# A row-sum kernel whose first buffer is filled by two loads, one row and then fifteen, rather than by one

## The chip, the cores and the metric

The kernel runs on one core of one Trainium2 chip (trn2). The metric is the device time of one execution in microseconds (us), lower is better. Before the change it was 163.97 us, the median of three runs (163.81 to 164.09).

## The reference

```python
batch, seq, dim = 32, 512, 1024            # x: float32, 67.1 MB
def reference(x):
    return np.sum(x, axis=-1).astype(np.float32)
```

Each of 16,384 rows of 1,024 numbers is summed. There is one addition per four bytes read, so the question is how fast 67.1 MB can be brought into the core's memory (SBUF).

## The kernel before

Each of the 128 partitions owns 128 consecutive rows. They are handled in eight tiles of 16 rows per partition (64 KiB per partition, 8 MiB per tile), in three rotating buffers. The vector engine (DVE) sums half of the rows of a tile in one instruction, the scalar engine (ACT) the other half row by row. The queue of SyncE (SP) issues all the loads.

```python
    def load(xt, c0, a, b):
        nc.sync.dma_start(out=xt[:, a:b], in_=x_p[:, c0 * D + a : c0 * D + b])
    # rows_dve: one tensor_reduce over n rows; rows_act: one activation with accumulation per row
    ...
    for t in range(T - 1):                        # seven whole tiles, G = 16 rows each
        c0 = t * G
        xt = xpool.tile([P, G * D], F32, tag="xt", name="xt")     # bufs=3
        load(xt, c0, 0, G * D)
        rows_dve(xt, c0, 0, G // 2)
        rows_act(xt, c0, G // 2, G // 2)
    # the last tile: loads of 8, 4, 2, 1 rows and three parts of a row, so that little work is left at the end
    ...
```

## Time and profile before

| what | number | read in |
|---|---|---|
| time | 163.97 us | runs |
| span of the profiled run | 162.4 us | page |
| busy: DVE, ACT | 69.9 us, 69.0 us | page, part 1 |
| whole tiles readable, steady part | every 19.36 us | timeline |
| one 8 MiB tile in 19.36 us | 8.389 MB / 19.36 us = 433 GB/s | worked out |

These are lines of the page of the kernel before: busy time per engine with its share of the span, the load queue (packets, MB, share of the time of 16 DMA engines), the chain of waits by engine, and the two costliest groups (busy us, mean ns of one, then idle time before them and what ended it).

```profile
DVE 69.9 (43%) x16; ACT 69.0 (43%) x129; POOL 0.2 (0%) x4
...
q1 hardware_dynamic: 2160, 67.18, 96.3%
...
DMA 85%; DVE 11%; SPq 1%; issue 1%; DVEq 0%
...
L43 DVE TENSOR_REDUCE res<-xt 128x8 f32<-128x8192 f32 (+3 forms) x10 | 68.7, 6873 | 89.0 <-DMA xt<-in_x_dram 89.0
L53 ACT ACTIVATE xt<-xt 128x1024 f32<-128x1024 f32 x64 | 66.7, 1043 | 89.3 <-DMA xt<-in_x_dram 89.1
```

Both compute engines are idle for more than half of the span, and it is a load that ends nearly all of it. The pace of the loads stands in the timeline of DVE before the change (start us, duration us, engine, line, operation, and in brackets the idle time before it and its releaser). Each line starts when a tile has landed.

```profile
22.97 8.69 DVE L43 TENSOR_REDUCE res<-xt 128x8 f32<-128x8192 f32 x1 [22.97 <-DMA xt<-in_x_dram]
42.27 8.69 DVE L43 TENSOR_REDUCE res<-xt 128x8 f32<-128x8192 f32 x1 [10.62 <-DMA xt<-in_x_dram]
...
100.73 8.69 DVE L43 TENSOR_REDUCE res<-xt 128x8 f32<-128x8192 f32 x1 [10.72 <-DMA xt<-in_x_dram]
120.09 8.69 DVE L43 TENSOR_REDUCE res<-xt 128x8 f32<-128x8192 f32 x1 [10.67 <-DMA xt<-in_x_dram]
139.44 8.69 DVE L43 TENSOR_REDUCE res<-xt 128x8 f32<-128x8192 f32 x1 [10.66 <-DMA xt<-in_x_dram]
```

From 100.73 to 120.09 and on to 139.44 is 19.36 and 19.35 us, of which DVE works 8.69. The Trainium skill (DMA: Bandwidth & Descriptors, section "Where 436 GB/s comes from") gives 435 GB/s as the ceiling of the path into SBUF; this trace's 433 GB/s agrees. In its middle the stream is therefore full.

The waits of SP's queue in the same kernel (what waited, for what: us in total, times, longest):

```profile
SPq L40 <- DVE res L43: 105.8, 5, 29.6
SPq L40 <- DMA xt<-in_x_dram: 7.8, 1, 7.8
```

The queue waits for a free buffer with two tiles of loads still in front of it: the time from issue to landing of a whole tile is 49.4 us, over two and a half tiles.

### The profile page before, as it was taken

The numbers are of one execution on the slowest core, as the hardware profiler recorded it, in microseconds if no ns is written. First come the engines' busy times: TensorE is split into PE (matmuls) and PEld (weight loads), VectorE is DVE, ScalarE is ACT, GpSimd is POOL, SyncE is SP. The second block draws the span as 40 slices with busy tenths as digits, with TensorE's granted clock in tenths as the row PEclk, the third lists the DMA queues.
The fourth block names the chain that finished last, engine by engine and source line by source line (L and its number), as shares of the span: only waits on it lengthen the run. The fifth ranks groups of instructions, "written<-read, shape, count | busy, mean of one in ns | idle before, by whom it ended". The sixth has DMA issues, their size and how long they took to land.

```text
span 162.4 us, 220 instructions
## 1 busy us (share of the span) xinstructions
DVE 69.9 (43%) x16; ACT 69.0 (43%) x129; POOL 0.2 (0%) x4
## 2 busy tenths in 40 slices
DVE  0000039700595007940099101990049700697882
ACT  3000039700594007930099101990039600696881
POOL 0000000000000000000000000000000000000000
DMA  7979989989989989989997997997997997999980
GB/s 258 517 323 452 517 355 420 517 371 404 501 355 436 517 371 404 517 371 404 517 452 325 517 468 307 517 468 323 501 484 323 484 484 307 452 420 408 418 350 20
DMA packets 2161, 67.18 MB, mean 414 GB/s; under 512 B 240, under 2 KB 624, under 8 KB 880
## 3 DMA queue, kind: packets, MB, share of 16 engines
q1 hardware_dynamic: 2160, 67.18, 96.3%
q14 instruction: 1, 0.01, 0.0%
HBM read 67.11 MB, written 0.07 MB: 414 GB/s over the span
## 4 chain that ended last, share of the span: by engine, by line
DMA 85%; DVE 11%; SPq 1%; issue 1%; DVEq 0%
DMA xt<-in_x_dram 85%; DVE res L43 11%; SPq L40 1%; DVE xt L62 0%; DVE part L62 0%; DVEq L62 0%; DVEq L128 0%
## 5 line engine op out<-in xcount | busy, mean ns | idle before, releaser
L43 DVE TENSOR_REDUCE res<-xt 128x8 f32<-128x8192 f32 (+3 forms) x10 | 68.7, 6873 | 89.0 <-DMA xt<-in_x_dram 89.0
L53 ACT ACTIVATE xt<-xt 128x1024 f32<-128x1024 f32 x64 | 66.7, 1043 | 89.3 <-DMA xt<-in_x_dram 89.1
L53 ACT ACTIVATION_READ_ACCUMULATOR xt<-xt 128x1 f32 x64 | 11.9, 187 | 0.0
L53 ACT ACT_TABLE_LOAD x1 | 1.3, 1283 | 0.7 <-PEq L117 0.7
L62 DVE CUSTOM_DVE_ANT_0 xt<-xt 128x256 f32<-128x256 f32 x1 | 0.4, 425 | 0.9 <-DMA xt<-in_x_dram 0.9
L62 DVE CUSTOM_DVE_ANT_0 xt<-xt,part 128x128 f32<-128x128 f32 x2 | 0.7, 352 | 0.1
L62 DVE DVE_READ_ACCUMULATOR2_ANT part<- 128x1 f32 x2 | 0.2, 82 | 0.0
L117 POOL MEMSET const-bfloat16-1.0<- 128x1 bf16 x1 | 0.1, 101 | 0.0
L117 POOL MEMSET const-uint8-127<- 128x1 uint8 x1 | 0.1, 101 | 0.0
L117 POOL MEMSET const-float32-0.0<- 128x1 f32 x1 | 0.1, 98 | 0.2 <-issue 0.2
L117 POOL MEMSET const-float32-1.0<- 128x1 f32 x1 | 0.1, 98 | 0.0
L62 DVE DVE_READ_ACCUMULATOR2_ANT res<- 128x1 f32 x1 | 0.1, 84 | 0.0
## 6 DMA issues: line engine op xcount, KB each, us to landing
xt<-in_x_dram SPq DMA_DIRECT2D x1, 4096.0 KB, 39.7
xt<-in_x_dram SPq DMA_DIRECT2D x1, 2048.0 KB, 44.2
xt<-in_x_dram SPq DMA_DIRECT2D x1, 1024.0 KB, 46.2
xt<-in_x_dram SPq DMA_DIRECT2D x1, 512.0 KB, 47.0
xt<-in_x_dram SPq DMA_DIRECT2D x1, 256.0 KB, 47.1
xt<-in_x_dram SPq DMA_DIRECT2D x2, 128.0 KB, 43.0
xt<-in_x_dram SPq DMA_DIRECT2D x7, 49.4
out_dram<-res SPq DMA_DIRECT2D x1, 64.0 KB, 1.5
```

Source lines behind the costliest of these rows:

```text
L40: nc.sync.dma_start(out=xt[:, a:b], in_=x_p[:, c0 * D + a : c0 * D + b])
L43: nc.vector.tensor_reduce(out=res[:, c0 + j : c0 + j + n], in_=xt[:, j * D : (j + n) * D].rearrange("p (j d) -> p j d", d=D), axis=mybir.A ...
L53: nc.scalar.activation(out=v, in_=v, func=mybir.ActivationFunctionType.Copy, accum_out=res[:, c0 + i : c0 + i + 1],)
L62: nc.vector.tensor_tensor_reduce(out=xt[:, a : a + h], in0=xt[:, a : a + h], in1=xt[:, a + h : b], scale=1.0, scalar=first, op0=ADD, op1=A ...
L117: nc = _bacc.Bacc("TRN2", target_bir_lowering=False, num_devices=1)
```

## The change

The first whole tile is loaded as row 0 and then rows 1 to 15. The intent of such a change is that something arrives early. The code after the loads is the same.

```diff
     for t in range(T - 1):
         c0 = t * G
         xt = xpool.tile([P, G * D], F32, tag="xt", name="xt")
-        load(xt, c0, 0, G * D)
+        if t:
+            load(xt, c0, 0, G * D)
+        else:
+            load(xt, c0, 0, D)
+            load(xt, c0, D, G * D)
         rows_dve(xt, c0, 0, G // 2)
         rows_act(xt, c0, G // 2, G // 2)
```

## The prediction

> **What bounds the kernel now.** The input stream bounds it. In the timeline, the full 8 MiB tiles become readable at 42.27, 61.96, 81.33, 100.73, 120.09 and 139.44 us, which in the steady part is 19.36 us apart: 8.389 MB / 19.36 us = 433 GB/s. The trace's packet records say the same of one engine: a 65,536-byte packet (one partition of one tile) takes 2.42 us, 27.1 GB/s, back to back, on 16 engines. This agrees with the 435 GB/s ceiling that the Trainium skill gives (DMA: Bandwidth & Descriptors, section "Where 436 GB/s comes from"), so the stream has nothing left to gain in its middle. The chain of waits gives 85% of 162.4 us to the loads. The reductions are short beside them: the table of groups has DVE 69.9 us and ACT 69.0 us busy, with 8.69 us of vector work per tile of 19.36 us; both engines stand idle for 89 us waiting for loads. With three buffers the loads are queued two to three tiles ahead (issue to landing: 49 us), so the issuing engine, whose waits for free buffers look long (105.8 us), holds nothing up.
>
> The ends of the stream: the first packets start about 1.7 us into the span, the 16 engines start over 1.17 us, and their first packets take 2.55 to 3.41 us rather than 2.42. The last load is read at 158.6 us and about 3.8 us of tail follow.
>
> **What the change does.** Same bytes, same reductions, one load more. The first 128 packets of 64 KiB become 128 packets of 4 KiB and 128 of 60 KiB. The first reduction on DVE reads rows of both loads and the ACT rows lie in the second, so no reduction can start before the whole first tile has landed. No work starts earlier, and the hidden reductions would not shorten the stream if it did.
>
> Costs:
> - One more issue on the queue of SP, 0.33 to 0.50 us in the timeline. The second load's issue should be over at about 1.6 us, before the first packet even starts; an engine has 8 small packets, at 0.16 us each 1.3 us, plus 0.5 to 1 us of first-packet delay, to hide it. No gap expected: 0 us.
> - Per-packet overhead. A 4 KiB packet took 0.160 us in the tail against 0.151 us at the steady rate, so 8 of them cost about 0.08 us more per engine; one more completion packet costs about 0.01 us. The timeline agrees: the tail's load of one row arrived about 1.28 us after the load before, against 19.36 / 16 = 1.21 us. All this is on the critical path: +0.1 us.
> - Semaphores: the loads rotate over a few; the last tile's last piece before waited 7.8 us on a landing. It shifts by one load and keeps some 38 us of lead: 0 us.
>
> **Predicted.** 163.97 + 0.1 = 164.1 us, range 163.7 to 164.6. Chances: faster by over 2% 0.01, within 2% 0.97, slower by over 2% 0.02.
>
> **What would show it.** One load issue more, at about 1.2 us; 2,304 packets in the load queue rather than 2,160; first reduction at 22.97 + 0.1 = about 23.1 us; all later arrivals 19.36 us apart and shifted by the same 0.1 us; DVE and ACT busy times unchanged; small packets at the start with no gap of over 0.3 us on an engine before its first 60 KiB packet.
>
> **What would make it wrong.** The second load's descriptors arriving late, which leaves every engine idle for up to 1 us at the start (+0.5%). The 60 KiB packets being cut into many smaller ones (up to +0.1 us per 8 cuts). A start with short packets that loses less of the first-packet delay would give back 0.5 us. None reaches 2%.

## The result, and the profile after

The changed kernel took 163.93 us (median of 4 runs, 163.86 to 164.08), the kernel before 163.95 us in its 4 runs. The ratio is 1.000 with a 95% interval of 0.9983 to 1.0017: the same.

The lines of the page after the change:

```profile
DVE 69.9 (43%) x16; ACT 69.0 (43%) x129; POOL 0.2 (0%) x4
...
q1 hardware_dynamic: 2304, 67.18, 96.5%
...
DMA 85%; DVE 11%; SPq 2%; issue 1%; DVEq 0%
```

Busy times are unchanged, the load queue has 2,304 packets (2,160 before: a packet is a piece that the records list with its own start, size and duration, here one partition's part of one load; 128 of the 144 more carry data, 16 have four bytes and mark the end of the added load), and the chain is the same but for the issue of one load more. The issue of the second load shows as its own piece in the chain of waits, in order of time, after the change (start us, us, what); it is over at 1.58 us:

```profile
0.73 0.38 SPq L40
1.11 0.05 issue
1.16 0.43 SPq L40
```

The timeline of DVE after the change:

```profile
22.88 8.69 DVE L43 TENSOR_REDUCE res<-xt 128x8 f32<-128x8192 f32 x1 [22.88 <-DMA xt<-in_x_dram]
42.18 8.69 DVE L43 TENSOR_REDUCE res<-xt 128x8 f32<-128x8192 f32 x1 [10.61 <-DMA xt<-in_x_dram]
...
100.75 8.69 DVE L43 TENSOR_REDUCE res<-xt 128x8 f32<-128x8192 f32 x1 [10.87 <-DMA xt<-in_x_dram]
120.10 8.69 DVE L43 TENSOR_REDUCE res<-xt 128x8 f32<-128x8192 f32 x1 [10.66 <-DMA xt<-in_x_dram]
139.44 8.69 DVE L43 TENSOR_REDUCE res<-xt 128x8 f32<-128x8192 f32 x1 [10.66 <-DMA xt<-in_x_dram]
```

The first tile came 0.09 us earlier, not 0.1 us later as predicted; by the fifth tile the two kernels are level. Nor were the arrivals in between 19.36 us apart, as predicted: after the second tile they came 19.56, 19.45 and 19.56 us apart. So the total fits, but not yet the reasons. One trace cannot decide about 0.1 us, so the experiments repeat both kernels, multiply the suspected cost, and move the small load.

### The profile page after: what moved, and what is told of

Same layout as the page of the kernel before. It is cut to its first block, busy times and chain, and to the rows that moved or that the text cites. A ratio compares the mean times of both kernels' runs of the same rounds, so it can differ in the third digit from the quotient of the medians.

```text
span 162.3 us, 224 instructions
## 1 busy us (share of the span) xinstructions
DVE 69.9 (43%) x16; ACT 69.0 (43%) x129; POOL 0.2 (0%) x4
## 3 DMA queue, kind: packets, MB, share of 16 engines
q1 hardware_dynamic: 2304, 67.18, 96.5%
## 4 chain that ended last, share of the span: by engine, by line
DMA 85%; DVE 11%; SPq 2%; issue 1%; DVEq 0%
DMA xt<-in_x_dram 85%; DVE res L43 11%; SPq L40 2%; DVE xt L62 0%; DVE part L62 0%; DVEq L62 0%; DVEq L132 0%
```

## The experiments

Four theories stood against each other. A: the prediction, a small cost per packet, all on the critical path, and nothing gained. B: the short packets also lose less at the start of the stream, and about 0.2 us comes back. C: splits cost nothing anywhere. And the reading that the change invites: an early first row lets work begin early.

To see the start closely, the packet records of each profile were added up as follows: 15 us after the first packet, how many bytes have landed (a packet in flight counts in proportion), and how much longer did that take than at 433.6 GB/s, the steady 27.1 GB/s of 16 engines? This "deficit" is in us; the same at 150 us shows what was lost on the whole way. These are own calculations from the records, one execution per line of the table, not lines of the profile.

| kernel | first load, then | deficit at 15 us | at 150 us | ratio to the kernel before (95% interval) |
|---|---|---|---|---|
| before, first trace | 16 rows | 1.04 | 1.21 | |
| before again | 16 rows | 1.14 | 1.24 | 1.0004 (0.9990 to 1.0019) |
| DVE work doubled | 16 rows | 1.13 | 1.20 | 0.9999 (0.9985 to 1.0013) |
| order reversed | 15 rows, 1 row | 1.14 | 1.22 | 0.9994 (0.9980 to 1.0007) |
| halves | 8 rows, 8 rows | 1.12 | 1.33 | 1.0001 (0.9988 to 1.0014) |
| two rows first | 2 rows, 14 rows | 0.85 | 1.11 | 0.9991 (0.9977 to 1.0005) |
| changed, first trace | 1 row, 15 rows | 0.86 | 1.40 | 1.0000 (0.9983 to 1.0017) |
| changed, second | 1 row, 15 rows | 0.90 | 1.18 | 0.9984 (0.9972 to 0.9997) |
| changed, third | 1 row, 15 rows | 1.09 | 1.12 | 0.9985 (0.9973 to 0.9998) |
| row 0 reduced early | 1 row, 15 rows | 0.88 | 1.44 | 0.9981 (0.9968 to 0.9995) |
| all seven tiles split | 1 row, 15 rows | 0.91 | 1.46 | 1.0014 (1.0001 to 1.0026) |
| ramp | 1, 2, 4, 9 rows | 1.27 | 1.54 | 1.0000 (0.9986 to 1.0014) |
| quarter row first | 1/4 row, 15 3/4 rows | 1.49 | 1.56 | 1.0022 (1.0009 to 1.0035) |
| sixteen loads | 16 times 1 row | 1.73 | 2.21 | 1.0116 (1.0084 to 1.0149) |

All outputs are right. The first four new runs shared one chip and its runs of the kernel before, likewise the next four and the last four.

### The kernel before, once more

No edit. The noise floor.

> The unchanged kernel once more, as the noise floor. Every theory: ratio 1.000 to the kernel before within 0.1%. Its packet records also show how much the loss in the first packets (0.53 us per engine in the first profile, beyond 2.42 us a packet) and the scattered long packets in the middle of the stream (0.16 us per engine) vary from one execution to the next. If the middle varies by 0.3 us or more with the same kernel, the longer middle of the changed kernel (0.54 us) is no effect of the change.

Measured: 164.11 us against 164.05 us, ratio 1.0004. The profiles of one and the same kernel put the first tile at 22.97 and 23.17 us, so a single first-tile time says nothing about 0.1 us. The deficit at 15 us was 1.04 and 1.14, and between 15 and 150 us 0.17 and 0.10 us were added: the middle varied by less than 0.1 us, not by 0.3 us. The three profiles of the changed kernel vary far more there, from 0.03 to 0.54 us, so by that measure too the longer middle of the first one is no sure effect of the change.

### The changed kernel, twice more

No edit against the changed kernel.

> The changed kernel once more, with more rounds. Theory A (the prediction): per-packet overhead of eight 4 KiB packets and one completion per engine, +0.08 to +0.1 us, all on the critical path, ratio 1.0005. Theory B: the short packets also lose less at the start, since the first-packet delay is paid beside a short packet instead of a long one, and give back 0.2 us: ratio 0.9990 to 1.0000, and the mean engine finishes the first tile 0.1 to 0.2 us earlier than in the kernel before, as it did in the first profile (20.38 against 20.22 us after the first packet). If that early finish doesn't repeat, B falls.

Measured: 163.88 us, ratio 0.9984 (0.9972 to 0.9997).

> The changed kernel a third time, beside the order-reversed one. The first 4 runs gave ratio 1.000, six more 0.9984 (0.9972 to 0.9997). Theory A in its recorded size (+0.08 to +0.1 us): 1.0005. Theory A with the size that the kernel with all tiles split shows (a split tile arrives 19.42 us after the one before against 19.36 us, so +0.06 us): 1.0004. Theory B (a gain of 0.2 us or more at the start on top): 0.9985 to 0.9995. At a noise of 0.1% a ratio of 0.9985 again would speak for B, one of 1.000 or more would leave nothing to explain.

Measured, on another chip: 163.82 us, ratio 0.9985 (0.9973 to 0.9998). Two calls of two agree on -0.15%, which is -0.25 us, while the first four runs showed 0.00%. The early finish of the first tile repeated in the deficit of the second profile (0.90) and hardly in the third (1.09). The gain of theory B is likely but small, and well inside what counts as the same.

### All seven whole tiles split

```diff
-        load(xt, c0, 0, G * D)
+        load(xt, c0, 0, D)
+        load(xt, c0, D, G * D)
```

> All seven whole tiles are loaded as 1 + 15 rows, not the first one alone. Theory A: each split costs 0.08 us more of stream (eight 4 KiB packets at 0.1595 us against 0.1511 us each, and a completion packet of 0.015 us), so seven cost +0.6 us: 164.5 us, ratio 1.0035. Theory B (gain at the start): six extra splits of the middle get nothing back, so +0.5 us over the changed kernel and +0.4 us over the kernel before. Theory C (the splits cost nothing anywhere, since the stream's pace is set by something other than packets): ratio 1.000.

Measured: 164.31 us, ratio 1.0014 (1.0001 to 1.0026). Theory A's +0.6 us is outside; nothing at all (C) is outside too, barely. Theory B's +0.4 us over the kernel before (ratio 1.0024) is inside. Against the changed kernel of the same call, six splits more cost 164.34 - 163.86 = 0.48 us in the means. The DVE timeline of this kernel gives the price of a split:

```profile
22.66 8.69 DVE L43 TENSOR_REDUCE res<-xt 128x8 f32<-128x8192 f32 x1 [22.66 <-DMA xt<-in_x_dram]
42.07 8.69 DVE L43 TENSOR_REDUCE res<-xt 128x8 f32<-128x8192 f32 x1 [10.73 <-DMA xt<-in_x_dram]
61.49 8.69 DVE L43 TENSOR_REDUCE res<-xt 128x8 f32<-128x8192 f32 x1 [10.73 <-DMA xt<-in_x_dram]
80.93 8.69 DVE L43 TENSOR_REDUCE res<-xt 128x8 f32<-128x8192 f32 x1 [10.75 <-DMA xt<-in_x_dram]
100.72 8.69 DVE L43 TENSOR_REDUCE res<-xt 128x8 f32<-128x8192 f32 x1 [11.11 <-DMA xt<-in_x_dram]
```

A split tile follows its predecessor by 19.41 and 19.42 us, where an undisturbed whole one takes 19.36: about 0.06 us per split, not the 0.08 to 0.1 us predicted. Of the four that follow, three came after 19.42 to 19.44 us and one after 19.79 us, a hiccup of the kind that the kernel before has too (19.69 us between 42.27 and 61.96). Six splits at 0.06 us are 0.36 us; the other 0.12 us of the 0.48 lie within the noise of these means (0.13% of 164 us is 0.2 us).

### The first tile in sixteen loads

```diff
         ...
+        else:
+            for r in range(G):
+                load(xt, c0, r * D, (r + 1) * D)
         ...
```

> The first tile is loaded as 16 loads of one row, 15 of them added. Theory A: 128 packets of 4 KiB per engine at 0.0084 us too much each make 1.07 us, 15 completions 0.2 us: +1.3 us, 165.2 us; with theory B's gain of 0.2 us at the start +1.1 us. Theory C: 0. If the issues of the loads (0.43 us each on the queue of SP, at most eight loads in flight) were what counts, gaps between packets of an engine would show in the first 20 us and the loss would be above 1.5 us.

Measured: 166.14 us, but spread from 164.99 to 166.91; ratio 1.0116. The profiled run was one of the shorter, 165.34 us. In its ACT timeline each row is taken up as it lands:

```profile
20.21 1.06 ACT L53 ACTIVATE xt<-xt 128x1024 f32<-128x1024 f32 x1
...
21.48 1.06 ACT L53 ACTIVATE xt<-xt 128x1024 f32<-128x1024 f32 x1
...
22.77 1.06 ACT L53 ACTIVATE xt<-xt 128x1024 f32<-128x1024 f32 x1
```

A row arrives every 1.28 us, against 19.36 / 16 = 1.21 us: 0.07 us per one-row load, and again somewhat less than the prediction's 0.09. The deficit gives less: between 10 and 15 us after the first packet, in which four rows' packets started, it grew by 0.17 us, 0.04 us per row. Sixteen such loads explain at most about 1.1 of the 1.9 us between the means (166.03 and 164.11). The rest is something else: between 5 and 15 us after the first packet the deficit grew from 0.93 to 1.73 us, and in that stretch the packet records hold 19 packets of 4 KiB that took 0.21 to 0.84 us instead of 0.16. What they took too long sums to 7.9 us, over 16 engines 0.49 us. SP did wait for landings before it could issue more (14 times, 65.4 us in the whole execution), but the records show no time there with fewer than 16 packets in flight, so the gap that a late issue would leave isn't seen, although the loss is above the 1.5 us that was expected of it. What makes these packets long, and why the runs of this kernel scatter by 1.9 us, stays open.

### The same two loads in the other order

```diff
         ...
+        else:
+            load(xt, c0, D, G * D)
+            load(xt, c0, 0, D)
         ...
```

> The same two loads of the first tile in the other order: 15 rows first, then the one row. Same packets, same count. Theory A: no different from the changed kernel, +0.06 us, ratio 1.0004. Theory B: the gain at the start needs the short packets to be the first, so it is gone here: 0.06 us slower than the kernel before and 0.2 to 0.3 us slower than the changed kernel in the same call (ratio to before 1.0004, while the changed kernel has 0.9985); the mean engine finishes the first tile as late after the first packet as in the kernel before (20.38 and 20.48 us) plus 0.06, not at 20.22.

Measured: 163.97 us, all five runs between 163.94 and 163.99; ratio 0.9994 (0.9980 to 1.0007). Its deficit at 15 us, 1.14 us, is that of the kernel before. The packets are the same as in the changed kernel, only their order differs, so in these traces the early gain goes with the order: it is there when the short packets come first. One trace of this order doesn't prove it, since the third trace of the changed kernel, at 1.09 us, is nearly as late. In time the difference to the changed kernel of the same call is 163.97 - 163.83 = 0.14 us in the means, less than the 0.2 to 0.3 us expected and not clear of the noise. The start of the packet records tells the same story: the first 60 KiB packets of this kernel took 2.86 to 3.30 us instead of 2.27.

### Row 0 reduced as soon as it lands

```diff
         ...
+            load(xt, c0, 0, D)
+            load(xt, c0, D, G * D)
+            rows_dve(xt, c0, 0, 1)
+            rows_dve(xt, c0, 1, G // 2 - 1)
         ...
```

> The changed kernel with the first reduction on DVE cut into row 0 alone and rows 1 to 7, so that row 0 is reduced as soon as its own load has landed: the first reduction starts at about 4.5 us rather than 22.9. If starting work early were worth something, the 1.2 us of that reduction would be gained: ratio 0.993. Theory of the prediction (the loads bound it and the reductions are hidden): the early start gains nothing, every later arrival stays 19.36 us apart, ratio 1.000 within 0.2% and no different from the changed kernel.

Measured: 163.80 us, ratio 0.9981 (0.9968 to 0.9995), which isn't to be told from the changed kernel's 0.9985. The DVE timeline of this kernel shows what the early start is worth:

```profile
4.15 1.22 DVE L43 TENSOR_REDUCE res<-xt 128x1 f32<-128x1024 f32 x1 [4.15 <-DMA xt<-in_x_dram]
22.71 7.62 DVE L43 TENSOR_REDUCE res<-xt 128x7 f32<-128x7168 f32 x1 [17.35 <-DMA xt<-in_x_dram]
42.08 8.69 DVE L43 TENSOR_REDUCE res<-xt 128x8 f32<-128x8192 f32 x1 [11.74 <-DMA xt<-in_x_dram]
```

The first reduction starts 18.7 us earlier than in the changed kernel. DVE then merely waits 17.35 us for the next load, and before the second tile it is idle for 11.74 us rather than 10.61: the work done early comes back as waiting. Early work is worth nothing here.

### The DVE work of six tiles done twice

```diff
         load(xt, c0, 0, G * D)
+        if t < 6:
+            rows_dve(xt, c0, 0, G // 2)
         rows_dve(xt, c0, 0, G // 2)
```

> The kernel before with the 8.69 us reduction on DVE done twice in six of the seven whole tiles (the second overwrites the first with the same sums), 52 us of work more. If the reductions were on the critical path, as the 11% of the chain of waits given to that line might be read, the time rises by up to 52 us. Theory of the prediction: 17.4 us of vector work per tile still fits under the 19.36 us between tiles, only the free buffer comes 8.7 us later and the loads are queued two tiles ahead: ratio 1.000 within 0.2%, arrivals still 19.36 us apart.

Measured: 164.05 us, ratio 0.9999. The page of this kernel (busy time per engine, then the chain of waits by engine) and its DVE timeline:

```profile
DVE 122.0 (75%) x22; ACT 69.0 (43%) x129; POOL 0.2 (0%) x4
...
DMA 74%; DVE 22%; SPq 1%; issue 1%; DVEq 0%
```

```profile
61.85 17.41 DVE L43 TENSOR_REDUCE res<-xt 128x8 f32<-128x8192 f32 x2 [1.95 <-DMA xt<-in_x_dram]
81.20 17.41 DVE L43 TENSOR_REDUCE res<-xt 128x8 f32<-128x8192 f32 x2 [1.94 <-DMA xt<-in_x_dram]
```

52 us of work more, no time more, and arrivals still 19.35 us apart. The chain of waits now gives DVE 22%: a chain may run through a reduction that frees a buffer although the stream has two tiles of loads queued in front of it. The share of a line in the chain is no price of that line.

### Other sizes of the first load

```diff
-        load(xt, c0, 0, G * D)
+        cuts0 = (...) if t == 0 else (0, G * D)     # (0, 8*D, G*D), (0, 2*D, G*D), (0, D, 3*D, 7*D, G*D), (0, D//4, G*D)
+        for a, b in zip(cuts0, cuts0[1:]):
+            load(xt, c0, a, b)
```

> The first tile in two loads of 8 rows each, so the first packets are 32 KiB. Ratios so far: 1 + 15 rows 0.9984 and 0.9985, 15 + 1 rows 0.9994. Theory B1 (what is lost at the start grows with the length of the first packets): half of the gain or less, ratio 0.9990 to 1.0000, first tile readable at about 23.1 us as in the kernel before. Theory B2 (any second load at the start gains, for instance by the engines' descriptors being handed over in smaller portions): as good as 1 + 15, 0.9985, first tile readable at about 22.9 us. Theory A, with no gain at the start, and the small cost of 32 KiB packets: 1.000.

Measured: 164.04 us, ratio 1.0001; the deficit, 1.12 us, is that of the kernel before. In this profile a second load alone gained nothing, which speaks against B2 and for short first packets; with one trace, and with ratios whose intervals overlap those of the changed kernel, it isn't proof. Of the half of the gain that B1 allowed, nothing is seen.

> First load of 2 rows, then 14: first packets of 8 KiB, whose overhead per byte is half that of 4 KiB. B1: nearly the whole gain, 0.9980 to 0.9990, first tile readable at 22.7 to 23.0 us. B2: 0.9985. A: 1.000. With the noise of 0.13% this cannot be told from 1 + 15 rows, but it must not be worse than 8 + 8 rows if B1 holds.

Measured: 163.83 us, ratio 0.9991 (0.9977 to 1.0005); deficit 0.85 us, first tile at 22.54 us. This speaks for B1 by the deficit; by time alone it is open.

> First tile in loads of 1, 2, 4 and 9 rows. In the kernel with 1 + 15 rows the first 60 KiB packets still took up to 0.3 to 0.6 us longer than 2.27 us on some engines. If a slow growth of the packets avoids that, 0.1 us more is gained: ratio 0.9975 to 0.9985, the best version so far. If the loss only moves, the ratio is as for 1 + 15 rows, 0.9985, or worse by the 0.06 us of each of the two loads added, 0.9990. Theory A: four loads cost 0.1 to 0.2 us, ratio 1.001.

Measured: 164.14 us, ratio 1.0000. The start was the best of all, a deficit of 0.79 us at 5 us after the first packet, but 0.48 us were lost between 5 and 15 us, the same stretch in which the kernel with sixteen loads had its slow packets. The loss only moved.

> First load of a quarter row (1 KiB packets, 8 per engine, about 0.4 us of transfer), then 15.75 rows. B1 alone: as good as 1 + 15 rows, 0.9980 to 0.9990. But the second load is issued 0.43 to 0.48 us after the first, which is now longer than the 0.4 us of transfer that has to cover it: if the interval between issues is exposed, each engine stands idle for up to 0.2 us between its last 1 KiB packet and its first long one, and the gain is gone: 0.9990 to 1.0000. Such a gap would show in the packet records.

Measured: 164.48 us, ratio 1.0022 (1.0009 to 1.0035), the one small variant that is clearly slower than the kernel before. Its deficit at 15 us is 1.49 us and its first tile is late:

```profile
23.58 8.69 DVE L43 TENSOR_REDUCE res<-xt 128x8 f32<-128x8192 f32 x1 [23.58 <-DMA xt<-in_x_dram]
```

The expected gap is there: counted from the records, 16 packets are in flight at once for the first time 1.92 us after the first packet, against 0.86 us in the first trace of the changed kernel and 1.17 us in that of the kernel before. Up to 5 us, what is missing from 16 packets in flight sums to 0.74 us per engine, against 0.47 and 0.51. That is about 0.25 us more idle than in these two traces, close to the 0.2 us expected of an exposed issue interval; the other profiles with short first packets have 0.20 to 0.39 us, so the size isn't settled. The other 0.2 to 0.4 us lie inside packets: some of the first long ones took 3 to 3.9 us instead of 2.38. Why those, no run here shows.

## Why the prediction was right

The predicted range of 163.7 to 164.6 us around 164.1 us held 163.93 us, and "within 2%" was right. The range was wide beside the +0.1 us forecast, so this alone proves little. Its points one by one:

- **What bounds the kernel.** Right, and shown by intervention: 52 us of extra DVE work cost nothing, and a reduction that starts 18.7 us earlier gains nothing. (The work of ACT was not varied.)
- **No work starts earlier.** Right: the first reduction started at 22.88 us instead of 22.97.
- **One more issue, hidden.** Right for this size: it was over at 1.58 us, before the first packet (about 1.7 us). Whether an engine had a gap before its first long packet can't be read, since the records don't name the engine; in all, 0.47 us per engine was idle in the first 5 us, against 0.51 us in the kernel before.
- **Semaphores, 0 us.** Nothing speaks against it: SP waited twice on a landing, 9.5 us in all, rather than once for 7.8 us, but between 15 and 150 us what was missing from 16 packets in flight is 0.02 us per engine in both first traces.
- **Per-packet overhead, +0.1 us.** Right in kind, too large: a split cost 0.06 us in the kernel with all tiles split, 0.04 to 0.07 us per one-row load in the kernel with sixteen.
- **The sign of the sum.** The prediction kept the first-packet delay out of its sum and named it among the risks, at 0.5 us. It probably belongs in the sum: among the profiles whose first load is one or two rows, and whose next is 14 or 15, the deficit at 15 us is 0.85 to 0.91 in five and 1.09 in one; in the five that start with 8 rows or more it is 1.04 to 1.14. In the means that is 0.92 against 1.11 us, 0.2 us less. The 0.06 us of the split fall within these 15 us and are already counted, so the term itself would be about -0.26 us (an estimate from these figures). A net of -0.2 us is a ratio of 0.9988; measured were 1.000, 0.9984 and 0.9985. By 150 us, however, the profiles no longer show it: the mean deficit is 1.29 us in the four that load 1 + 15 rows in the first tile alone, and 1.24 us in the five with long starts. So the predicted +0.1 us is not borne out, a gain of 0.2 us at the start is likely, and what of it reaches the total is not shown. The mis-sized step is this one, a term left at 0; the range covered it, and the fit of the total is in part luck.

Where the gain of 0.2 us goes in the first trace also shows in the table: that profile lost 0.54 us between 15 and 150 us, the kernel before 0.17. The other profiles of one-row starts lost 0.28, 0.03 and 0.56 there, those of long starts 0.07 to 0.21. It may be that the start is partly paid for later, but the third profile speaks against a rule, and no run here settles it. In the first trace 0.45 of the 0.54 us were lost between 40 and 80 us after the first packet, in later tiles whose loads are the same in both kernels. Nor do the runs show fully why a first packet of 32 KiB or more costs more than one of 4 or 8 KiB. One part can be seen: 16 packets are in flight at once 0.44 to 0.86 us after the first packet in the profiles that start with one or two rows (the one with sixteen loads not counted), and 0.89 to 1.47 us in those that start with eight or more. But two short packets of one engine may be counted as two engines here, and the split of the deficit between late engines and long packets varies between traces as much as it differs between the kernels.

No variant beats the changed kernel clearly; all that are faster than the kernel before are so by 0.2% or less.

## What to carry to other kernels

When a stream of loads already runs at its full rate and the compute hides below it, ask of a change to the loads only what it does to the first microseconds, the last ones and the packets between; an earlier first result is worth nothing unless someone was waiting for it. Multiply a suspected cost, here by splitting all tiles, before you believe its size: 0.1 us in one place can't be seen, and seven of them can. Short first packets won back about 0.2 us at the start of the stream in most profiles here, which is too little to show in the time for certain; a quarter of a row, or sixteen small loads in a row, cost more than they brought.

## What the Trainium skill lacked or had wrong

- DMA: Bandwidth & Descriptors, section "Bandwidth", advises at least 1 MiB per load and shows 341 GB/s for a load of that size (measured on the other kind of issue, from GpSimd). It has no figure for loads under 1 MiB in a full queue: here loads of 0.5 MiB arrived every 1.28 us in the kernel with sixteen, which is 0.524 MB / 1.28 us = 410 GB/s.
- The same page has no figure for the start of a stream. In the first trace of the kernel before, the first 16 packets began within 1.17 us and took 2.55 to 3.41 us instead of 2.42, and in the profiles with long first packets the start cost 1.04 to 1.14 us against the full rate, or 0.85 to 0.91 us in most profiles with short first packets.
- The same page's first-byte latency for loads issued from SP, about 0.6 us (section "Latency and other measured facts"), agrees only when it is counted from the end of the issue: that ended at 1.10 us and the first packet began at about 1.7 us, 1.0 us after the issue began at 0.73 us.
- Its ceiling of 435 GB/s (section "Where 436 GB/s comes from") agrees with the trace: 433 GB/s. The same section says that for transfers between HBM and SBUF the HBM side, at about 358 GB/s, is the limit; these loads come from HBM, with one core at work, and ran at 433 GB/s.
